# Seven slots of 4 KB in place of five in the ring of a two-layer decoder's weight and modulation loads

## The chip, the cores and the metric

The kernel runs on one core of a Trainium2 chip. The metric is the time of one execution on the device in microseconds; the median of three runs before the change is 2487.04 us (2481.87 to 2489.46).

## What is computed

A trunk of two decoder layers for one sequence of 256 tokens of width 2048, in fp32. Layer 0 mixes tokens by gated linear attention (GLA), layer 1 by forgetting attention (FoX); each mixer is followed by a gated MLP of inner width 5632 with a causal convolution of width 3. Every sub-layer is normalised and then shifted, scaled and gated by vectors that come from a conditioning vector `c` through large matrices `w_mod`:

```python
cond = jax.nn.silu(c)
for i in range(DEPTH):
    mod = (cond @ w_mod[i] + b_mod[i])[:, None, :]
    sh_m, sc_m, g_m, sh_f, sc_f, g_f = jnp.split(mod, 6, axis=-1)
    h = rmsnorm(x, norm_mix[i]) * (1.0 + sc_m) + sh_m
    ...
    x = x + (1.0 + g_m) * y
    h = rmsnorm(x, norm_ffn[i]) * (1.0 + sc_f) + sh_f
    x = x + (1.0 + g_f) * conv_ffn(h, ffn_w_up[i], ffn_conv_w[i], ffn_conv_b[i], ffn_w_down[i])
return rmsnorm(x, norm_final)
```

With one sequence of 256 tokens every weight is read from HBM once and used for 256 columns of TensorE.

## The kernel before

**Weights.** All projections run as a stream of weight tiles of 128 rows by 1024 columns in fp32: 512 KB each, 4 KB in every partition. The list `plan` holds the tiles of the whole kernel in the order of use. `next_w` (line 503) gives out the next one. It keeps `AHEAD` = 3 tiles beyond the current one already split, and loads tiles ahead of the next split up to `look` = `RING` - 1 of them (line 507); for the first three tiles `look` is 1 (lines 508 and 509). A load is a DMA on SP's queue (line 519) into a slot of the pool `ring`:

```python
wt = ringt([P, 1024])
...
run, look = AHEAD if hold is None else hold, RING - 1
...
while fetched["load"] < min(fetched["split"] + look, len(plan)):
```

**The split.** `split_w` (line 109) makes two fp32r tiles of a weight tile: ScalarE casts it to `wh` (line 114), VectorE subtracts that from the weights for `wl` (line 115). VectorE's subtraction is the last reader of the slot, so it frees the slot. Operands `h` or `op` are split in the same way, and each product is three matmuls, of the high parts and the two mixed ones: 24 matmuls of 256 columns for a tile in `stream_a` (lines 549 to 551), 12 of 512 in `stream_b` (lines 582 to 584).

**Modulation.** The matrices `w_mod` do not go through TensorE for the most part. Their tiles, also 512 KB, lie in slots of the same pool `ring` (lines 230 and 233), and VectorE adds each one, scaled by a column of `c`, to an accumulator (line 254), which frees the slot. When the 16 tiles of a chunk of columns are done, TensorE transposes the accumulator (line 267) and ScalarE or VectorE sums it up. `tick` (line 318) runs after every weight tile: it has up to `PEND` = 2 modulation loads given out ahead (`prefetch`, line 307), and carries out accumulations at a pace set for each stage. `drain_bg` (line 336) works off what is left before a norm needs it. The first modulation tiles, up to the first block of the norm, are wide ones of 1 MB in another pool, `big`.

**Other users of the ring.** The rows of gains (line 141), the biases (line 178), the convolution's weights (line 188) and the gate's weights (line 674) lie in slots of the ring for a while.

**Order.** The program is written in one order of Python calls; a planner with costs of its own arranges each engine's instructions and gives out slots and semaphores. `issue_after` (as in `after_startup`, line 212, for the first `SLOAD` = 12 loads) adds an order by hand: those loads come after the last wide one in SP's queue. SP, VectorE and ScalarE each work their instructions off in order.

**Memory.** `RING` = 5 (line 31) is the number of slots (line 80). Line 1256 opens the program with a scratch of 8192 bytes in each partition for the descriptors of dynamic DMAs.

Of the kernel before, what the change touches and what calls it, by code (L numbers as in the profile page):

```python
# [27 lines left out]
GH = 4  # L28
FH = 16
SECT = {"sh_m": 0, "sc_m": 1, "g_m": 2, "sh_f": 3, "sc_f": 4, "g_f": 5}  # L30
RING = 5
AHEAD = 3
DIRECT = 4
XAFTER = 1
# [33 lines left out]
def kernel(  # L68
# [10 lines left out]
    const = ctx.enter_context(tc.tile_pool(name="const", bufs=1))  # L79
    ring = ctx.enter_context(tc.tile_pool(name="ring", bufs=RING))  # L80
    big = ctx.enter_context(tc.tile_pool(name="big", bufs=NBIG))
# [421 lines left out]
    def next_w(kt, cols, hold=None):  # L503
        i = fetched["use"]
        assert plan[i][1] == kt and plan[i][3] == tuple(cols), (plan[i][1:], kt, cols)
        fetched["use"] += 1
        run, look = AHEAD if hold is None else hold, RING - 1
        if i < STAGE:
# [760 lines left out]
```

## Time and profile before

| | |
|---|---|
| median of three runs | 2487.04 us |
| profiled execution | 2483.4 us, its span 2481.7 us |
| granted TensorE clock, mean | 0.982 |
| busy: TensorE, VectorE, ScalarE | 2419.4, 1905.7, 1281.2 us |
| moved by DMA | 638.36 MB, 257 GB/s over the span |

The page gives one execution, taken by the hardware profiler. PE is TensorE's matmuls, DVE VectorE, ACT ScalarE, SPq the sequencer of SyncE, which gives out the DMAs. `L115` is line 115 of the kernel; `wl<-w,wh` are the tiles that an instruction writes and reads. A line of waits names who waited and, behind the arrow, what ended the wait. Matmuls are pipelined and their ends are modelled, so a busy share of TensorE is not a rate; the number of its instructions in a window is.

### The profile page before, as it was taken

To read this page: it belongs to the slowest core of one execution; us is meant where nothing else is said; L and a number is where in the kernel's file an instruction comes from. 1 tells how busy PE (TensorE), PEld (TensorE's weight loads), DVE (VectorE), ACT (ScalarE), POOL (GpSimd) and SP (SyncE) were. 2 spreads that over 40 slices of the span, in tenths; PEclk is the share of its full clock that TensorE was granted. 3 is DMA by queue.
4 is the path that set the end of the run, shared out by engine and by line. 5 is a ranking of instruction groups with operands and counts; after the bars stand their busy time and mean duration, and the time that the engine had idled before them with its cause. 6 is when DMAs were issued, how large, how long until landed. Compare 5 with 4: busy or idle time off the path is not lost.

```text
span 2481.7 us, 47540 instructions
## 1 busy us (share of the span) xinstructions
PE 2419.4 (97%) x19226; PEld 2331.5 (94%) x19226; DVE 1905.7 (77%) x2560; ACT 1281.2 (52%) x1956; POOL 15.7 (1%) x35
## 2 busy tenths in 40 slices
PE   6999999899999999999999999999999999999998
PEld 6988899899999999999988888999999999999998
DVE  6777989787789999877587888877776777767544
ACT  2446554344655666543454555554655556565433
POOL 0000000000000000000000000000000000000000
PEclk7999999899999999999999999999999999999999
DMA  8897878798668988899589887787677777766553
GB/s 349 274 311 241 294 260 289 252 323 310 207 195 267 313 313 300 280 316 314 183 267 310 303 284 243 234 274 264 200 236 234 231 235 233 230 195 218 191 192 123
DMA packets 184313, 638.36 MB, mean 257 GB/s; under 512 B 23961, under 2 KB 24971, under 8 KB 183708
## 3 DMA queue, kind: packets, MB, share of 16 engines
q1 hardware_dynamic: 183704, 635.17, 77.2%
q8 instruction: 150, 2.46, 0.4%
q14 instruction: 71, 0.58, 0.1%
q10 hardware_dynamic: 388, 0.15, 0.0%
HBM read 633.14 MB, written 2.10 MB: 256 GB/s over the span
## 4 chain that ended last, share of the span: by engine, by line
PE 77%; DMA 11%; DVE 8%; issue 3%; ACT 2%; DVEq 0%; SPq 0%; ACTq 0%
PE pa L549 20%; PE pa L551 20%; PE pa L550 20%; DMA wm<-in_w_mod_dram 7%; PE pa L583 4%; PE pa L582 4%; PE pa L584 4%; DVE wl L115 3%; DVE acc L254 3%; DMA w<-in_ffn_w_down_dram 2%; DMA w<-in_gla_w_out_dram 1%; ACT wh L114 1%; DMA w<-in_gla_w_in_dram 1%; PE pm L267 1%; PE pm L416 0%
## 5 line engine op out<-in xcount | busy, mean ns | idle before, releaser
L114 ACT CAST wh<-w 128x1024 fp32r<-128x1024 f32 x819 | 856.5, 1048 | 1033.9 <-PE pa L550 486.1
L115 DVE TENSOR_TENSOR wl<-w,wh 128x1024 fp32r<-128x1024 f32 x819 | 996.2, 1221 | 369.8 <-ACT wh L114 359.4
L549 PE MATMUL pa<-h,wh 128*128 128x256 f32 x3584 | 990.7, 278 | 7.6 <-ACT h L470 5.7
L550 PE MATMUL pa<-h,wh 128*128 128x256 f32 x3584 | 992.9, 278 | 1.0 <-DVE h L472 1.0
L551 PE MATMUL pa<-h,wl 128*128 128x256 f32 x3584 | 992.3, 278 | 1.2 <-DVE wl L115 1.2
L549 PEld LDWEIGHTS pa<-h,wh 128*128 128x128 f32 x3584 | 673.7, 189 | 9.4 <-ACT h L470 6.6
L551 PEld LDWEIGHTS pa<-h,wl 128*128 128x128 f32 x3584 | 674.9, 189 | 3.9 <-issue 2.3
L550 PEld LDWEIGHTS pa<-h,wh 128*128 128x128 f32 x3584 | 676.1, 189 | 2.0 <-DVE h L472 1.7
L254 DVE SCALAR_TENSOR_TENSOR acc<-wm,cT,acc 128x1024 f32<-128x1024 f32 x352 | 451.8, 1283 | 117.8 <-DMA wm<-in_w_mod_dram 116.0
L549 PE MATMUL pa<-op,wh 128*128 128x256 f32 x1920 | 527.8, 278 | 6.2 <-ACT wh L114 3.1
L550 PE MATMUL pa<-op,wh 128*128 128x256 f32 x1920 | 527.6, 277 | 0.0
L551 PE MATMUL pa<-op,wl 128*128 128x256 f32 x1920 | 518.2, 279 | 2.6 <-DVE wl L115 1.7
L549 PEld LDWEIGHTS pa<-op,wh 128*128 128x128 f32 x1920 | 361.8, 189 | 7.6 <-ACT wh L114 4.3
L550 PEld LDWEIGHTS pa<-op,wh 128*128 128x128 f32 x1920 | 362.5, 189 | 0.0
L551 PEld LDWEIGHTS pa<-op,wl 128*128 128x128 f32 x1920 | 355.2, 189 | 5.7 <-DVE wl L115 5.7
L583 PE MATMUL pa<-wh,h 128*128 128x512 f32 x512 | 201.4, 395 | 0.0
L582 PE MATMUL pa<-wh,h 128*128 128x512 f32 x512 | 199.8, 394 | 0.3 <-ACT wh L114 0.3
L584 PE MATMUL pa<-wl,h 128*128 128x512 f32 x512 | 192.5, 393 | 0.8 <-DVE wl L115 0.8
L582 PEld LDWEIGHTS pa<-wh,h 128*128 128x128 f32 x512 | 96.7, 189 | 20.2 <-ACT wh L114 0.7
L583 PEld LDWEIGHTS pa<-wh,h 128*128 128x128 f32 x512 | 96.6, 189 | 19.6 <-issue 0.2
L584 PEld LDWEIGHTS pa<-wl,h 128*128 128x128 f32 x512 | 95.7, 188 | 20.4 <-DVE wl L115 1.5
L1049 ACT ACTIVATE y<-u,cw 128x256 f32<-128x256 f32 x176 | 101.7, 600 | 11.1 <-DVE act L1065 8.6
(237 smaller groups left out, 1387.0 us busy)
## 6 DMA issues: line engine op xcount, KB each, us to landing
wm<-in_w_mod_dram SPq DMA_DIRECT2D x352, 512.0 KB, 5.1
w<-in_ffn_w_up_dram SPq DMA_DIRECT2D x320, 512.0 KB, 4.5
w<-in_ffn_w_down_dram SPq DMA_DIRECT2D x176, 512.0 KB, 4.6
w<-in_fox_w_in_dram SPq DMA_DIRECT2D x128, 512.0 KB, 4.8
w<-in_gla_w_in_dram SPq DMA_DIRECT2D x96, 512.0 KB, 5.0
wm<-in_w_mod_dram SPq DMA_DIRECT2D x16, 1024.0 KB, 12.2
w<-in_gla_w_out_dram SPq DMA_DIRECT2D x32, 512.0 KB, 5.4
w<-in_ffn_w_up_dram SPq DMA_DIRECT2D x64, 256.0 KB, 4.0
```

The source lines that it names most:

```text
L114: nc.scalar.copy(out=hi, in_=src)
L115: order["v"] = nc.vector.tensor_tensor(out=lo, in0=src, in1=hi.bitcast(F32), op=ALU.subtract).ins
L254: nc.vector.scalar_tensor_tensor(out=st["a"], in0=wt[:, j, :], scalar=col, in1=st["a"], op0=ALU.mult, op1=ALU.add)
L267: nc.tensor.transpose(pt[:, m * P:(m + 1) * P], st["a"][:, (q0 + m) * P:(q0 + m + 1) * P], ident)
L549: nc.tensor.matmul(o, wh[:, ms], rh, start=(first and m % 2 == 0), stop=False, skip_group_check=True)
L550: nc.tensor.matmul(o, wh[:, ms], rl, start=False, stop=False, skip_group_check=True)
L551: nc.tensor.matmul(o, wl[:, ms], rh, start=False, stop=last, skip_group_check=True)
L582: nc.tensor.matmul(o, lh[:, ts_], wh[:, hs_], start=first, stop=False)
L583: nc.tensor.matmul(o, ll[:, ts_], wh[:, hs_], start=False, stop=False)
L584: nc.tensor.matmul(o, lh[:, ts_], wl[:, hs_], start=False, stop=last)
L1049: nc.scalar.activation(y, u, AF.Identity, scale=cw[:, l * 3 + 2, r:r + 1], bias=cw[:, 6 + l, r:r + 1])
```

## The change

The ring has seven slots in place of five. The same constant is in `next_w`, so weights are loaded up to six tiles ahead of the split in place of four. The scratch for dynamic DMAs is 1024 bytes in place of 8192.

```diff
-RING = 5
+RING = 7
 AHEAD = 3
...
-    nc = _bacc.Bacc("TRN2", target_bir_lowering=False, num_devices=1, dynamic_dma_scratch_size=8192)
+    nc = _bacc.Bacc("TRN2", target_bir_lowering=False, num_devices=1, dynamic_dma_scratch_size=1024)
```

## Rows read from the trace of the kernel before

**Rows 1.** The page: busy time by engine, and the DMA queues (packets, MB, share).

```profile
PE 2419.4 (97%) x19226; PEld 2331.5 (94%) x19226; DVE 1905.7 (77%) x2560; ACT 1281.2 (52%) x1956; POOL 15.7 (1%) x35
...
q1 hardware_dynamic: 183704, 635.17, 77.2%
q8 instruction: 150, 2.46, 0.4%
q14 instruction: 71, 0.58, 0.1%
q10 hardware_dynamic: 388, 0.15, 0.0%
```

**Rows 2.** Windows: busy (x instructions) PE, PEld, DVE, ACT, POOL; clock, DMA share, GB/s.

```profile
400.00:450.00 50.00, 48.53 (x404) 46.53 (x403) 43.77 (x50) 21.08 (x37) 0.00 (x0) 1.00 0.91 310
450.00:500.00 50.00, 42.35 (x293) 40.46 (x291) 38.12 (x66) 21.18 (x40) 0.00 (x0) 0.80 0.69 233
2100.00:2150.00 50.00, 50.00 (x444) 50.00 (x443) 38.36 (x51) 26.73 (x34) 0.00 (x0) 1.00 0.75 237
```

**Rows 3.** Windows around the end of the GLA output projection, same columns.

```profile
415.00:465.00 50.00, 48.39 (x394) 45.98 (x394) 42.12 (x45) 21.17 (x36) 0.00 (x0) 1.00 0.96 333
465.00:475.00 10.00, 7.11 (x36) 6.22 (x35) 6.45 (x6) 3.13 (x3) 0.00 (x0) 0.71 0.94 343
475.00:485.00 10.00, 8.84 (x65) 8.56 (x64) 6.31 (x15) 7.14 (x23) 0.00 (x0) 0.84 0.43 125
485.00:495.00 10.00, 6.54 (x30) 6.24 (x31) 7.82 (x26) 3.31 (x7) 0.00 (x0) 0.50 0.17 47
505.00:515.00 10.00, 10.00 (x91) 10.00 (x90) 10.00 (x14) 4.66 (x6) 0.00 (x0) 1.00 0.92 315
```

**Rows 4.** ScalarE's wait, 390 to 480 us: total, times, longest.

```profile
ACT wh L114 <- DMA w<-in_gla_w_out_dram: 40.1, 22, 4.3
```

**Rows 5.** TensorE's waits over the span; VectorE's timeline at 1107.

```profile
PE pm L267 <- DVE acc L254: 8.0, 4, 3.8
PE pa L549 <- ACT wh L114: 3.1, 4, 1.7
PE pa L549 <- DVE xT L605: 3.0, 1, 3.0
PE pa L551 <- DVE wl L115: 3.0, 5, 1.2
PE pa L584 <- DVE wl L115: 0.8, 1, 0.8
...
1107.44 1.28 DVE L254 SCALAR_TENSOR_TENSOR acc<-wm,cT,acc 128x1024 f32<-128x1024 f32 x1 [2.54 <-DMA wm<-in_w_mod_dram]
```

**Rows 6.** SP's waits: span, 57 to 66 us; then its timeline.

```profile
SPq L519 <- DVE wl L115: 964.0, 460, 19.9
SPq L233 <- DVE wl L115: 355.2, 284, 18.1
...
SPq L233 <- DVE wl L115: 18.8, 2, 18.1
...
43.94 22.14 SPq L233 DMA_DIRECT2D wm<-in_w_mod_dram  x3
```

**Rows 7.** Windows of the start-up and first stretch, same columns.

```profile
20.00:50.00 30.00, 23.11 (x109) 21.14 (x108) 26.54 (x43) 8.56 (x16) 0.23 (x2) 0.70 1.03 409
57.00:65.00 8.00, 4.50 (x18) 3.81 (x19) 6.53 (x15) 5.17 (x8) 0.00 (x0) 0.50 0.00 1
65.00:200.00 135.00, 128.89 (x917) 120.60 (x916) 98.51 (x103) 60.17 (x85) 0.00 (x0) 0.98 0.89 300
```

**Rows 8.** DMA issues, 390 to 480, then 2300 to 2440: KB, us to landing.

```profile
w<-in_gla_w_out_dram SPq DMA_DIRECT2D x23, 512.0 KB, 5.3
...
w<-in_ffn_w_down_dram SPq DMA_DIRECT2D x51, 512.0 KB, 3.6
```

## The prediction

> **What bounds the kernel now.** I read the page's shares first. TensorE is busy 97% of a span of 2481.7 us [rows 1], which looks as if nothing could be gained. That share is a union of modelled ends, so the number of matmuls in equal windows comes next: 444 in 50 us is the engine's own pace with 256 columns, 0.113 us each, and it is held in nearly all windows from 650 us on; 400 to 500 us hold 404 and 293 [rows 2]. So the kernel is bound by TensorE in its later part, and falls short of TensorE's pace in a few stretches before about 1130 us. Where the columns allow a comparison, the largest shortfall is the end of the GLA output projection [rows 3]: 394 matmuls in 415 to 465 us where 452 fit at 505 to 515's 91 (rounded to 90.5 per 10 us), and 36 in 465 to 475 where 90.5 fit. That is 58 + 54.5 matmuls by 0.1105 us, 12.4 us. There the DMA engines are 96% busy at 333 GB/s, and ScalarE's casts wait 40.1 us for that projection's weights [rows 4].
>
> TensorE's own waits name two kinds of lateness [rows 5]. Late weights: 3.1 us on the casts and 3.0 + 0.8 us on the low parts. Late modulation: 8.0 us in four waits on the accumulator that the transposes at the end of a chunk read, and 3.0 us on the residual of the FFN's down projection, which in VectorE's order stood behind an accumulation that had waited 2.54 us for its modulation tile [rows 5]. In sum 11.0 us. VectorE works in order, so a late modulation tile also holds up the split of weights that have landed.
>
> The load queue's waits show what feeds this [rows 6]. SP waits 964.0 us before weight loads and 355.2 us before modulation loads until VectorE's split (line 115) frees a slot. Most of this is harmless: TensorE has all it needs. Not harmless is the 18.8 us up to 66 us: five slots are full, nothing is freed until the first split, and from 57 to 65 us the DMA engines stand at 0.00 [rows 7], after which 65 to 200 us run at 0.89 of the DMA engines. A second row says whether more loads in flight could be served faster: from 20 to 50 us, with the wide 1 MB loads queued, the same engines moved 409 GB/s [rows 7], against 333 with five slots of 512 KB [rows 3].
>
> **The change, part by part.** *Instructions.* No arithmetic, no DMA and no byte is added or removed. ScalarE's casts and VectorE's subtractions stay as many as they are. Cost 0, and it needs no cover.
>
> *The smaller scratch.* Every transfer in the table of queues is on a hardware queue or an instruction queue [rows 1]; nothing there would use a dynamic scratch. I take 0. Two slots take 8192 bytes of a partition, the scratch gives 7168, so 1024 come from free space, and tiles get other addresses; no row prices an address, and I take 0 with 2 us each way.
>
> *Look-ahead of six.* From the fourth tile on, SP is given weight loads six tiles ahead of the split in place of four. They overtake in SP's order the modulation loads of up to two ticks, and the gate, bias and convolution loads at their places. A tile of weights costs TensorE 24 matmuls, 2.7 us; a transfer at 333 GB/s costs 524 KB / 333 = 1.57 us, so two slots are 3.1 us of DMA time of head start, once in each stretch that the DMA engines limit, and only if there was idle DMA time before it.
>
> *Late weights, 415 to 475 us.* Lower bound: the head start alone, 3.1 us. Upper bound: all 12.4 us, if seven loads in flight come nearer to 409 GB/s. This stretch asks for a weight and a modulation tile per 2.7 us, 1.05 MB / 2.7 = 388 GB/s. The row of the stretch itself is at 0.96 of the engines, the other is of larger loads: I take 6.
>
> *Late weights elsewhere.* 3.0 + 0.8 us of waits on the low parts, of which a head start covers most: I take 2 (0 to 3.8).
>
> *Late modulation.* The modulation loads are still given out two ahead, so the slots do not move them by themselves. For: between 44 and 66 us the second and third modulation load wait for a slot [rows 6], and with seven they go at once, in the idle 8 us. Against: every later modulation tile may stand behind two more weights in one queue. Bounds: a gain of all 11.0 us, or a loss of five waits (four and one) by 3.1 us, 15.5 us. I take a gain of 3.
>
> *The clock.* The granted clock falls to 0.71 in 465 to 475 us and 0.84 in the next 10 us, and is 0.50, 1.2 GHz, in 485 to 495 us [rows 3]. TensorE had starved just before it fell. In 475 to 485 us 65 matmuls ran where 90.5 fit, 2.8 us, but the norm's own pause lies in it too. I take 1 (0 to 2.8).
>
> Sum: 6 + 2 + 3 + 1 = 12 us. The profiled execution took 2483.4 us, 3.6 under the median of the runs shown; 2483.4 - 12 = 2471.4, and by the median 2487.0 - 12 = **2475 us**. About 0.3%, 7.5 us, is what a measurement of this kernel can tell from no change, so the forecast is "faster", by not much more than that.
>
> The Trainium skill (DMA: Bandwidth & Descriptors, the note on 436 and 360 under its measured figures) says that between HBM and SBUF the HBM side binds, at about 358 GB/s per core. By that limit 333 would leave an estimated 7%, and the term of 6 would be near its lower end, some 3.1; the sum would be 9. The trace does not agree for this core running alone: it shows 409 GB/s from 20 to 50 us [rows 7].
>
> What is late next: where the weights are no longer late, the modulation tile is, since it has no slot of its own and lead no longer than before. After about 1130 us nothing can be gained, since TensorE already holds its pace.
>
> **The rivals.** *No change.* The extra slots hold weights that have landed and wait; the loads in flight stay as they are, since a slot is freed at VectorE's pace, and the DMA engines at 0.96 have little left. Then only head starts count, 3.1 us in 415 to 475 and about 2 elsewhere: 2487 - 5 = 2482 us. For it: the 0.96, and that SP's 964.0 us are mostly harmless. Against: 57 to 65 us at 0.00, and 409 GB/s.
>
> *Slower: modulation behind two more weights.* Its place is SP's one queue in the stretches where the DMA engines are full; its price 3.1 us at each of the five waits counted above, 15.5 us, less the 5 us of head starts: 2487 + 10 = 2497 us. It decides if the loads in flight fill up with weights, so that a modulation load's time from issue to landing grows by two transfers while its lead does not. For it: only the weights' look-ahead was raised. Against: there is one slot too few for four weights and two modulation tiles now, and one too few for six and two afterwards, so the slots, not the look-ahead, still ration SP.
>
> *Larger gain.* If seven in flight reach some 390 GB/s, the first stretches become TensorE's: 12.4 + 3.8 + 11.0 - some 2 for the residual that waits on other work, and 2.8 of clock, 28 us: 2459 us. For it: 409 GB/s, and that at low load a 512 KB transfer lands in 3.6 us against 5.3 here [rows 8], so latency counts. Against: every step must go right.
>
> *It does not do what it says.* A planner that prices instructions fixes the order on each engine; it might give the slots out in another order, with small changes either way. That is within the range.
>
> **How the numbers follow.** Forecast 0.46, no change 0.28, slower 0.14, larger gain 0.12. Faster by over 0.3%: the forecast's half above 7.5 us and more, 0.43, and the larger gain, 0.12: 0.55. Within 0.3%: the no-change case and the forecast's lower end, 0.31. Slower by over 0.3%: 0.14. The range runs from 2458, the larger gain, to 2492, the lower half of the slower case: it leaves out about 0.1 above and some 0.05 below. Both signs are not near balance, so the forecast's own range, 2468 to 2482, is told only for reading.
>
> **What would show it.** Right: the DMA engines at work in 57 to 65 us; casts waiting under 20 us for the output projection's weights; over 425 matmuls where 394 were; TensorE's waits on the low parts near 0. The forecast is wrong if these waits shrink and the span does not (the waits on the accumulator have grown: the slower case), if GB/s from 415 to 465 us stays at 333 with the same count of matmuls (no change), or if the time moves after 1130 us, where I see no cause.

## The result, and the profile after

The changed kernel takes 2471.31 us (median of four runs, 2467.44 to 2475.57) against 2487.78 us. The medians differ by 16.5 us; the measured ratio is 0.9943 with a 95% interval of 0.9928 to 0.9958, 14 us less, and the text goes by it. The forecast was 12 us less. The profiled execution took 2469.58 us, its span is 2467.9 us.

Windows of the kernel after, columns as in [rows 2]; they answer to [rows 3] and [rows 7]:

```profile
57.00:65.00 8.00, 4.34 (x17) 3.64 (x18) 6.53 (x15) 5.34 (x8) 0.00 (x0) 0.50 0.20 81
65.00:200.00 135.00, 129.46 (x920) 120.83 (x920) 97.01 (x101) 61.41 (x85) 0.00 (x0) 0.99 0.90 295
415.00:465.00 50.00, 50.00 (x444) 50.00 (x443) 46.93 (x51) 21.96 (x37) 0.00 (x0) 1.00 0.99 371
465.00:475.00 10.00, 7.53 (x53) 7.21 (x52) 5.19 (x11) 7.56 (x23) 0.00 (x0) 0.84 0.69 214
475.00:485.00 10.00, 5.95 (x28) 5.60 (x29) 7.28 (x28) 2.93 (x6) 0.00 (x0) 0.50 0.07 15
485.00:495.00 10.00, 10.00 (x88) 10.00 (x87) 10.00 (x20) 5.11 (x7) 0.00 (x0) 0.98 0.86 280
```

From 415 to 465 us TensorE now runs at its pace, 444 matmuls where 394 ran, and the DMA engines move 371 GB/s at 0.99 where they moved 333 at 0.96. The granted clock falls as before, but around the norm alone: it is back at 0.98 in 485 to 495 us, where it was 0.50. In the start-up little has moved: 0.20 of the DMA engines in 57 to 65 us, and 295 GB/s afterwards where 300 were.

TensorE's waits after, which answer to [rows 5], and ScalarE's from 390 to 480 us, which answers to [rows 4]:

```profile
PE pm L267 <- DVE acc L254: 9.7, 4, 5.2
...
PE pa L551 <- DVE wl L115: 3.6, 4, 1.2
...
PE pa L549 <- DVE xT L605: 2.1, 1, 2.1
...
PE pa L584 <- DVE wl L115: 0.2, 1, 0.2
```

```profile
ACT wh L114 <- DMA w<-in_gla_w_out_dram: 13.4, 8, 2.2
```

The casts wait 13.4 us for the output projection's weights in place of 40.1, and TensorE's 3.1 us of waits on the casts are gone. The waits on the accumulator are 9.7 us for 8.0; that is no difference by itself, since the kernel of the first experiment, which is the kernel before with another scratch, shows 10.0. VectorE's own waits on modulation did grow (121.4 us in that kernel); first before, then after:

```profile
DVE acc L254 <- DMA wm<-in_w_mod_dram: 116.0, 105, 3.4
```

```profile
DVE acc L254 <- DMA wm<-in_w_mod_dram: 139.9, 118, 4.1
```

So weights come earlier and modulation later. Where the time went is read from the same instructions in both timelines: the first matmul of the narrow gate product in GLA's second block (line 596), the first and the last matmul of the GLA output projection (lines 549 and 551), the broadcast for the norm of the first FFN (line 374), and the first matmul of FoX's narrow product (line 596). Before, then after:

```profile
209.95 0.28 PE L596 MATMUL pm<-h,wh 128*128 128x256 f32 x1
...
377.95 0.28 PE L549 MATMUL pa<-op,wh 128*128 128x256 f32 x1
...
479.96 0.28 PE L551 MATMUL pa<-op,wl 128*128 128x256 f32 x1
...
487.32 0.80 PE L374 MATMUL pm<-dg,ones 128*128 128x128 f32 x2 [2.82 <-DVE dg L372]
...
1239.10 0.58 PE L596 MATMUL pm<-h,wh 128*128 128x256 f32 x1 [2.58 <-ACT h L470]
```

```profile
212.21 0.28 PE L596 MATMUL pm<-h,wh 128*128 128x256 f32 x1
...
378.28 0.28 PE L549 MATMUL pa<-op,wh 128*128 128x256 f32 x1
...
467.14 0.28 PE L551 MATMUL pa<-op,wl 128*128 128x256 f32 x1
...
478.27 0.77 PE L374 MATMUL pm<-dg,ones 128*128 128x128 f32 x2 [2.91 <-DVE dg L372]
...
1226.42 0.58 PE L596 MATMUL pm<-h,wh 128*128 128x256 f32 x1 [3.24 <-ACT h L470]
```

Up to the first mark the change lost 2.3 us; from there to the norm it gained 11.3 (9.0 in all), up to FoX 3.6 more (12.7 in all), and 1.1 behind it, 13.8 us of span. The output projection takes 88.9 us in place of 102.0, so 13.1 us are gained inside it, and 3.8 are given back between its end and the norm's broadcast.

How far two traces of one program differ is shown by the kernel with the scratch alone: it comes to the first mark, the norm and FoX 1.2, 2.4 and 6.9 us later than the kernel before, and its output projection takes 101.9 us. So the 2.3 us lost at the first mark are hardly more, and the 3.6 us gained up to FoX are less, than what two such traces differ by there; the 13.1 us of the projection are far more.

### The profile page after: what moved, and what is told of

Same layout as the page of the kernel before. It is cut to its first block, busy times and chain, and to the rows that moved or that the text cites. A ratio compares the mean times of both kernels' runs of the same rounds, so it can differ in the third digit from the quotient of the medians.

```text
span 2467.9 us, 47315 instructions
## 1 busy us (share of the span) xinstructions
PE 2408.5 (98%) x19226; PEld 2325.8 (94%) x19226; DVE 1901.3 (77%) x2560; ACT 1283.2 (52%) x1956; POOL 14.8 (1%) x35
## 4 chain that ended last, share of the span: by engine, by line
PE 86%; DMA 6%; DVE 5%; issue 2%; ACT 1%; DVEq 0%; SPq 0%; ACTq 0%
PE pa L551 23%; PE pa L549 23%; PE pa L550 23%; DMA wm<-in_w_mod_dram 6%; PE pa L584 4%; PE pa L582 4%; PE pa L583 4%; DVE wl L115 2%; DVE acc L254 2%; PE pm L267 1%; PE pm L416 0%; PE pm L786 0%; ACT pt L276 0%; PE pt L267 0%; ACT wh L114 0%
## 5 line engine op out<-in xcount | busy, mean ns | idle before, releaser
L254 DVE SCALAR_TENSOR_TENSOR acc<-wm,cT,acc 128x1024 f32<-128x1024 f32 x352 | 451.1, 1281 | 141.0 <-DMA wm<-in_w_mod_dram 139.9
L551 PE MATMUL pa<-op,wl 128*128 128x256 f32 x1920 | 524.7, 277 | 0.0
```

The costliest lines, as they stand in the source:

```text
L254: nc.vector.scalar_tensor_tensor(out=st["a"], in0=wt[:, j, :], scalar=col, in1=st["a"], op0=ALU.mult, op1=ALU.add)
L551: nc.tensor.matmul(o, wl[:, ms], rh, start=False, stop=last, skip_group_check=True)
```

## The experiments

Each kernel was timed against the kernel before on the same chip, which came out at 2484 to 2486 us in these comparisons. Diffs are against the changed kernel, but for the first. "Left" is the number of slots minus the weights' look-ahead, what the look-ahead leaves in the ring for modulation.

| slots | look-ahead | left | median us | ratio to before, 95% interval | VectorE waits on modulation (line 254) |
|---|---|---|---|---|---|
| 5 | 6 | -1 | 2618.49 | 1.0532 (1.0509 to 1.0556) | 307.3 us |
| 5 | 4 (before) | 1 | 2487.78 | 1 | 116.0 |
| 6 | 5 | 1 | 2474.43 | 0.9953 (0.9937 to 0.9969) | 139.7 |
| 7 | 6 (after) | 1 | 2471.31 | 0.9943 (0.9928 to 0.9958) | 139.9 |
| 5 | 3 | 2 | 2466.28 | 0.9923 (0.9910 to 0.9937) | 22.0 |
| 7 | 5 | 2 | 2453.43 | 0.9876 (0.9862 to 0.9889) | 34.3 |
| 7 | 4 | 3 | 2449.85 | 0.9855 (0.9833 to 0.9877) | 7.4 |
| 8 | 5 | 3 | 2453.81 | 0.9875 (0.9860 to 0.9891) | 5.9 |
| 7 | 3 | 4 | 2451.22 | 0.9867 (0.9850 to 0.9883) | 1.8 |
| 8 | 4 | 4 | 2446.65 | 0.9847 (0.9834 to 0.9861) | 2.9 |

The traces also tell who holds the slots. A load takes a slot when SP gives it out, and the last instruction of VectorE that reads it (line 115 or 254) frees it. Counted so, with loads and these instructions paired in their order, the mean numbers of slots held are:

| slots, look-ahead | 75 to 195 us: weights, modulation | 405 to 440 us: weights, modulation |
|---|---|---|
| 5, 4 (before) | 3.30, 1.68 | 2.44, 2.55 |
| 7, 6 (after) | 5.28, 1.70 | 3.67, 3.30 |
| 7, 4 | 4.79, 2.16 | 3.16, 3.83 |
| 6 and 2 for modulation alone, 6 | 5.99, 1.99 | 5.99, 1.99 |

The first window lies ahead of GLA's second block: there both new slots of the change went to weights. The second lies in the output projection.

**The scratch alone** (against the kernel before).

```diff
-... dynamic_dma_scratch_size=8192)
+... dynamic_dma_scratch_size=1024)
```

> Five slots and a look-ahead of four as before, only the scratch is 1024 bytes. Theory F (seven loads in flight are served faster, 333 to 371 GB/s at the end of the GLA projection) and theory H (weights further ahead of the split when a crowded stretch begins) both expect no change: 2487 us, within 0.3%, 394 matmuls and about 333 GB/s from 415 to 465 us. Theory P (the smaller scratch, through addresses or the planner's order, is worth part of the gain) expects 2471 to 2480 us.

Measured: 2486.27 us, ratio 1.0002 (0.9990 to 1.0014), and 393 matmuls from 415 to 465 us:

```profile
415.00:465.00 50.00, 48.02 (x393) 45.76 (x393) 42.89 (x46) 19.99 (x35) 0.00 (x0) 1.00 0.95 330
```

The scratch, and the addresses with it, are worth nothing that can be told, 0.14% at most; theory P is out. VectorE waits 121.4 us on modulation here and TensorE 10.0 us on the accumulator, against 116.0 and 8.0 before.

**Seven slots, the look-ahead of before.**

```diff
-        run, look = AHEAD if hold is None else hold, RING - 1
+        run, look = AHEAD if hold is None else hold, RING - 3
```

> Seven slots, weights looked ahead four as before. Theory F: the two free slots go to modulation loads as well as weights, so as many loads are in flight; most of the gain stays, 2470 to 2475 us, at least 360 GB/s and over 430 matmuls from 415 to 465 us. Theory H: without the longer look-ahead the weights are as late as before; 2482 to 2489 us, about 394 matmuls there.

Measured: 2449.85 us, ratio 0.9855. Neither theory had room for that: by the medians it is 36 us faster than before, and 21 us faster than the change. The marks of this kernel:

```profile
200.60 0.28 PE L596 MATMUL pm<-h,wh 128*128 128x256 f32 x1
...
465.48 0.80 PE L374 MATMUL pm<-dg,ones 128*128 128x128 f32 x2 [2.82 <-DVE dg L372]
...
1204.71 0.58 PE L596 MATMUL pm<-h,wh 128*128 128x256 f32 x1 [2.70 <-ACT h L470]
```

By the first mark, where the change had lost 2.3 us, it has gained 9.4; by the norm 21.8, by FoX 34.4. The output projection runs from 366.0 to 458.9 us, 92.9 us: at the same look-ahead the two slots shorten it by 9.1 us, and the longer look-ahead of the change by 4.0 more. Theory F's other signs did not come: 387 matmuls and 328 GB/s from 415 to 465 us, but the projection ends inside that window. VectorE's waits:

```profile
DVE acc L254 <- DMA wm<-in_w_mod_dram: 7.4, 12, 1.1
```

116.0 and 139.9 us have become 7.4. Two of the seven slots, taken from the weights' look-ahead, made modulation punctual. On balance the longer look-ahead is a loss of 21 us inside the gain: it is worth 4 us in the output projection and costs more elsewhere.

**Five slots, the look-ahead of the change.**

```diff
-RING = 7
+RING = 5
...
-        run, look = AHEAD if hold is None else hold, RING - 1
+        run, look = AHEAD if hold is None else hold, RING + 1
```

> Five slots, weights looked ahead six. Theory F: five loads in flight at most, so nothing gained, 2484 to 2495 us, and more of the slots hold weights, so TensorE's waits on the accumulator grow from 8.0 us. Theory H: weights further ahead gain on the projections, 2475 to 2482 us.

Measured: 2618.49 us, ratio 1.0532. Theory H falls; F had the side right and the size far too small. VectorE's waits, then TensorE's:

```profile
DVE acc L254 <- DMA wm<-in_w_mod_dram: 307.3, 191, 5.1
```

```profile
PE pa L551 <- DVE wl L115: 34.8, 36, 2.6
PE pm L267 <- DVE acc L254: 31.1, 11, 4.5
```

The ring's slots fill with weights whose turn has not come, and modulation gets fewer of them: 1.29 on average from 75 to 195 us, where it held 1.68 before. TensorE waits on the accumulator 31.1 us, and on the low parts, which stand behind it in VectorE's order, 34.8. This is the rival that the prediction called slower, with nothing to pay for it.

**Six slots, look-ahead five.**

```diff
-RING = 7
+RING = 6
```

> Six slots, look-ahead five. Both F and H expect about half of the change's 16 us: 2477 to 2482 us, and 410 to 435 matmuls from 415 to 465 us. If one more slot already lifts the stretch to TensorE's pace, it takes nearly all of it, 2471 to 2475 us.

Measured: 2474.43 us, ratio 0.9953, whose interval overlaps the change's.

```profile
415.00:465.00 50.00, 49.34 (x426) 48.53 (x425) 43.28 (x46) 20.54 (x37) 0.00 (x0) 1.00 0.96 341
```

426 matmuls and 341 GB/s stand between before and after, as F and H expected. The time misses their 2477 to 2482 us: it is nearly the change's own, as was expected only if one more slot lifted the stretch to TensorE's pace, which it did not.

After these four, theory S took the place of F and H: what counts first is what the look-ahead leaves.

**Five slots, look-ahead three.**

```diff
-RING = 7
+RING = 5
...
-        run, look = AHEAD if hold is None else hold, RING - 1
+        run, look = AHEAD if hold is None else hold, RING - 2
```

> Five slots as before the change, weights looked ahead three in place of four. Theory S (what decides is the number of slots that the weights' look-ahead leaves free for modulation, slots minus look: 1 before and after the change, 3 in the fast variant) gives it 2 and expects it faster than before with no slot added: 2458 to 2475 us, VectorE's waits on modulation under 60 us where they were 116. Theory T (seven slots are what pays, because more loads are in flight) expects 2484 us or more, since weights are looked ahead less and no slot is added.

Measured: 2466.28 us, ratio 0.9923, as S expected, and 22.0 us of waits on modulation, so theory T is out. One constant, and no byte of memory, gives about what the change gives with 8 KB more in every partition. ScalarE still waits for weights:

```profile
ACT wh L114 <- DMA w<-in_ffn_w_down_dram: 96.4, 60, 3.5
ACT wh L114 <- DMA w<-in_ffn_w_up_dram: 73.8, 51, 3.1
```

Before, these two waits were 85.1 and 45.9 us, and 89.2 and 81.5 in the kernel with the scratch alone, so the shorter look-ahead shows no clear cost there. After the change they are 3.2 and 5.0 us: that is what the two further slots pay for, and the ring gains from both.

**Seven slots, look-ahead five.**

```diff
-        run, look = AHEAD if hold is None else hold, RING - 1
+        run, look = AHEAD if hold is None else hold, RING - 2
```

> Seven slots, weights looked ahead five: two slots are left beyond the look-ahead. Theory S: between look 6 (2471) and look 4 (2450), nearer the fast end, 2451 to 2460 us, VectorE's waits on modulation 10 to 60 us. Theory T: the look-ahead matters little with seven slots once one is free; that would have shown at look 6 already, so 2465 us or more would speak for a threshold at three free slots.

Measured: 2453.43 us, ratio 0.9876; VectorE waits 34.3 us on modulation. Both lie in S's ranges: by the ratios the second slot left is worth some 17 us at seven slots, the third some 5, though the intervals with two and with three left overlap.

**Eight slots, look-ahead four.**

```diff
-RING = 7
+RING = 8
...
-        run, look = AHEAD if hold is None else hold, RING - 1
+        run, look = AHEAD if hold is None else hold, RING - 4
```

> Eight slots, weights looked ahead four: four slots beyond the look-ahead. Theory S: modulation can be two ahead, and seven slots already hold four weights, the two and one in use, so the eighth is worth nothing: 2446 to 2452 us. Theory T: another slot in flight gains again, 2435 to 2445 us.

Measured: 2446.65 us, ratio 0.9847, the fastest of all; its interval overlaps that of seven slots and four, so the eighth slot is worth at most a few us, as S expected.

**Modulation three ahead.**

```diff
-PEND = 2
+PEND = 3
...
-        run, look = AHEAD if hold is None else hold, RING - 1
+        run, look = AHEAD if hold is None else hold, RING - 3
```

> Seven slots, look-ahead four, modulation loads given out three ahead in place of two. Theory S: four weights and three modulation tiles just fill seven slots, one less is spare; VectorE's waits on modulation are 7.4 us without it, so there is little to gain and little to lose, 2445 to 2456 us. If the third tile takes a slot that the weights want, late weights come back: 2456 to 2466 us.

Measured: 2451.47 us, ratio 0.9868 (0.9854 to 0.9881), the same as without the third tile. With slots left over, giving the loads out earlier adds nothing.

**Slots of their own for modulation, weights six ahead; then weights four ahead.** Both take modulation out of the ring into a pool of two slots; the ring has six slots with the look-ahead of six, or five with four.

```diff
-RING = 7
+RING = 6
...
+    modp = ctx.enter_context(tc.tile_pool(name="modp", bufs=2))
...
-                st[kt] = bigt([P, per, width], "wm") if wide else ringt([P, per, width], "wm")
+                st[kt] = bigt([P, per, width], "wm") if wide else modp.tile([P, per, width], F32, tag="wm", name=nm("wm"))
...
-        run, look = AHEAD if hold is None else hold, RING - 1
+        run, look = AHEAD if hold is None else hold, RING
```

> Weights looked ahead six as in the change, in a ring of six that they have to themselves; modulation has two slots of its own. Theory S1 (a look-ahead of six harms because landed weights sit in the slots that modulation needs): with its own two slots modulation is never crowded out, 2444 to 2453 us, VectorE's waits on modulation under 40 us. Theory S2 (it harms because modulation's loads stand behind more weights in SP's queue, whatever the slots): 2460 to 2473 us, waits on modulation over 80 us.

In the second kernel `RING` is 5 and `look` stays `RING - 1`.

> Seven slots in all: weights have the five of before with the look-ahead of four, modulation has two of its own. S1 and S2 both expect the fast end, 2444 to 2456 us, near the shared seven with look-ahead four (2450 us).

Measured: 2464.23 us, ratio 0.9918 (0.9901 to 0.9934), and 2466.40 us, ratio 0.9923 (0.9904 to 0.9943). By its time the first lies in S2's range. VectorE's waits on modulation, 52.3 us in the first and 54.2 in the second, lie between S1's 40 and S2's 80. The second misses what both expected, so neither theory had the case right. TensorE's waits from 440 to 505 us, of the first and of the second kernel:

```profile
PE pm L268 <- DVE acc L255: 10.5, 1, 10.5
```

```profile
PE pm L268 <- DVE acc L255: 11.1, 1, 11.1
```

Each has one long wait on the accumulator ahead of the first FFN's norm (lines are one further down here), 10.5 and 11.1 us. The first one's timeline of SP shows why (the second's is alike):

```profile
455.49 0.33 SPq L190 DMA_DIRECT2D crow<-in_ffn_conv_w_dram  x1
455.87 0.46 SPq L191 DMA_DIRECT2D crow<-in_ffn_conv_b_dram  x1
457.47 12.20 SPq L234 DMA_DIRECT2D wm<-in_w_mod_dram  x5
485.32 7.22 SPq L520 DMA_DIRECT2D w<-in_ffn_w_up_dram  x5
```

The last five modulation loads went out after the convolution's weights: two slots did not let them keep up with the weights while these ran ahead, and the drain before the norm waited for them. In the shared ring of seven with look-ahead four no modulation load is left by then:

```profile
445.32 5.78 SPq L519 DMA_DIRECT2D w<-in_ffn_w_up_dram  x4
451.97 0.33 SPq L189 DMA_DIRECT2D crow<-in_ffn_conv_w_dram  x1
452.35 0.46 SPq L190 DMA_DIRECT2D crow<-in_ffn_conv_b_dram  x1
453.38 3.84 SPq L519 DMA_DIRECT2D w<-in_ffn_w_up_dram  x3
470.34 2.21 SPq L233 DMA_DIRECT2D wm<-in_w_mod_dram  x2
```

What the pair does tell: once modulation has its own slots, weights six ahead are not slower than four ahead, and VectorE waits on modulation as long. That speaks against the place in SP's queue as the cause, and for the slots; it is not a clean proof, since the two kernels also differ by one slot for weights. The count of slots explains why two of its own are not enough: in the shared ring of seven with look-ahead four, modulation holds 3.83 slots on average from 405 to 440 us and never under three. A pool of three or four was not tried.

**Eight slots, look-ahead five.**

```diff
-RING = 7
+RING = 8
...
-        run, look = AHEAD if hold is None else hold, RING - 1
+        run, look = AHEAD if hold is None else hold, RING - 3
```

> Eight shared slots, weights looked ahead five, three beyond the look-ahead. If slots minus look decides, as good as seven with four: 2445 to 2452 us. If a longer look-ahead harms by itself, nearer to seven with five: 2452 to 2456 us.

Measured: 2453.81 us, ratio 0.9875 (0.9860 to 0.9891), in the range of the second expectation, although VectorE's waits on modulation are 5.9 us. The interval overlaps that of seven with four, so the times alone do not tell them apart. The traces do, at one place. TensorE's waits from 440 to 505 us:

```profile
PE pm L416 <- ACT pm L276: 4.3, 1, 4.3
```

The norm's sum waits 4.3 us there for ScalarE, which sums up the last modulation chunk; with seven and four that wait is 0.7 us. ScalarE's timeline, here and then with seven and four, shows why:

```profile
460.77 1.98 ACT L114 CAST wh<-w 128x1024 fp32r<-128x1024 f32 x2
...
462.93 1.03 ACT L114 CAST wh<-w 128x1024 fp32r<-128x1024 f32 x1
...
464.27 0.26 ACT L276 ACTIVATE pm<-pm 128x128 f32<-128x128 f32 x1
```

```profile
460.60 0.26 ACT L276 ACTIVATE pm<-pm 128x128 f32<-128x128 f32 x1
...
461.39 2.92 ACT L114 CAST wh<-w 128x1024 fp32r<-128x1024 f32 x3
```

Three casts of the next projection's weights stand ahead of the last sums here, and behind them there. From the last matmul of the output projection to the norm's broadcast it takes 13.7 us here and 6.6 with seven and four. The same holds in all kernels here where modulation shares the ring: with a look-ahead of five or six three casts come ahead of the last sums and it takes 10.0 us or more (11.1 after the change), with three or four they come behind and it takes 6.6 to 7.4. So the slots left do not decide alone: at this norm a look-ahead of five or six costs some 3 to 7 us, whatever is left. That order of ScalarE's work was not changed by itself.

**Seven slots, look-ahead three.**

```diff
-        run, look = AHEAD if hold is None else hold, RING - 1
+        run, look = AHEAD if hold is None else hold, RING - 4
```

> Seven shared slots, weights looked ahead three, four beyond the look-ahead. Modulation is not late at look-ahead four already (7.4 us), so a shorter one can only make weights later: ScalarE's casts wait more for FFN weights, as they did with five slots and three (73.8 and 96.4 us); 2452 to 2465 us. If only the slots left over matter: 2444 to 2452 us.

Measured: 2451.22 us, ratio 0.9867, the same as look-ahead four within the intervals, and in the range for the case that only the slots left matter. VectorE's waits, then ScalarE's:

```profile
DVE acc L254 <- DMA wm<-in_w_mod_dram: 1.8, 2, 0.9
```

```profile
ACT wh L114 <- DMA w<-in_ffn_w_down_dram: 17.1, 11, 2.7
```

The casts do wait longer for the down projection, 17.1 us where it is 8.4 with look-ahead four, but TensorE does not feel it: its waits on the casts are 0.5 us here and 1.8 with four. At seven slots any look-ahead of three to five does; six does not.

## Why the prediction was right, and where it was not

The time was right, 14 us less where 12 were forecast, and so was the reading of what bounds the kernel: all but 1.1 us of the gain lies before FoX, at 1226 us. Two of its four terms were not, and that the sum came so near is in part luck: the term for late weights was some 3 us too small, and the 3 us for modulation did not come.

**Late weights, 415 to 475 us.** The mechanism held; the term was taken at 6 of 3.1 to 12.4 us. From the first matmul of the output projection to the norm's broadcast 9.4 us were gained: 13.1 inside the projection, over the upper bound, less what was given back ahead of the norm, where the changed kernel too has three casts ahead of ScalarE's last sums. I sat nearer to the row of the stretch itself, 0.96 of the engines, and it was the other end that decided: with two more slots the engines moved 371 GB/s.

**Late weights elsewhere.** Taken at 2; 3.6 us were gained between the norm and FoX, no more than two traces of one program differ by there (4.5 us), so the size is not shown. The waits on the low parts that I took it from did not shrink (3.0 and 0.8 us before, 3.6 and 0.2 after).

**Late modulation.** Taken as a gain of 3; none came. The step that failed is "with seven they go at once, in the idle 8 us". The three loads did go early, as SP's timeline after the change shows against [rows 6]:

```profile
44.04 5.43 SPq L233 DMA_DIRECT2D wm<-in_w_mod_dram  x3
64.78 3.72 SPq L519 DMA_DIRECT2D w<-in_gla_w_in_dram  x4
```

But all were given out by 49.5 us, SP then stood before a weight load until the first split had freed a slot, at 64.8 us, and the stretch behind it, which modulation limits, ended 2.3 us later, where the kernel with the scratch alone ended it 1.2 later. In that stretch the two new slots went to weights, and modulation held 1.70 slots where it had held 1.68. My sentence against it, that modulation tiles may stand behind more weights, was the one that came true, by the slots if not by the queue: VectorE's waits went from 116.0 to 139.9 us. What there was to gain is shown by the kernels with two slots or more left for modulation: they end that stretch 8 to 9 us earlier than before.

**The slower rival.** It was given 0.14, and its harm is at work in the changed kernel: at seven slots a look-ahead of six costs 21 us against four. I had placed it in SP's queue; the experiments speak for the slots, and for the order of ScalarE's work at the first FFN's norm. I had priced it at the five waits of TensorE, 15.5 us, and set 5 us of gain beside it; the slots' own gain is 36 us, since five slots had already let modulation be late. My argument against the rival counted the slots rightly, one too few before and after, and read it as harmless. With three left in place of one, FoX begins 34.4 us earlier than before.

**The rest.** Of the signs named, the casts' wait (13.4 us) and the matmuls (444) came; the DMA engines' work from 57 to 65 us hardly did (0.20), and the waits on the low parts did not go near 0. The scratch at 0 is confirmed (1.0002). Nothing moved after 1226 us but 1.1 us. The clock's term of 1 us can't be told from the weights' in these runs. The rival of no change rested on the DMA engines having little left at 0.96; they had 333 to 371 GB/s.

## What to carry to other kernels

When two streams share a ring, look at what the look-ahead of the one leaves to the other: a look-ahead written as the ring's size less one hands every new slot to the first stream, as the count of slots shows. Try the number of slots and the look-ahead apart; here one constant without memory gave as much as the whole change, and both together two and a half times as much. The sign here was VectorE: its waits for the second stream's loads grew while ScalarE's for the first one's shrank. And look at the order on each engine afterwards, since a longer look-ahead also moved casts ahead of work that the next norm needed.

## What the runs showed of the hardware

512 KB loads on one queue came to the rate of the start-up, where I had thought its 409 GB/s might need the 1 MB ones: from 415 to 465 us 333 GB/s before and 371 after, and with eight slots and look-ahead five, from 445 to 455 us:

```profile
445.00:455.00 10.00, 10.00 (x91) 10.00 (x90) 9.89 (x10) 2.56 (x3) 0.00 (x0) 1.00 1.03 404
```

404 GB/s at 1.03 of the engines, so the 333 of before was no limit of the memory for this core running alone. From the loads given out from 415 to 465 us and their median time from issue to landing (31 at 5.2 to 5.4 us before, 35 at 5.9 to 7.3 after) I estimate 3.3 loads in flight before and 4.5 after. That the rate grew because of them is not shown by itself: in single slices of 1.25 us of that window the kernel before moved up to 416 GB/s too.

The Trainium skill (DMA: Bandwidth & Descriptors, the note on 436 and 360) has the HBM side bind at about 358 GB/s per core, which it works out as half of a stack's 716. The traces of this core running alone do not agree, with 371 and 404.
